# Three plain gate/up pairs a layer instead of four, with the low parts of three operand preparations made by ScalarE and adding DMAs, and weight chunks loaded several to a transfer

## The chip, the cores and the metric

The kernel runs on one core of a Trainium2 chip. The metric is the device time of one execution in microseconds (us), the median of several runs; less is better. The core has five engines that run side by side, each with an instruction stream of its own: TensorE (PE in the profile, with its weight loads as PEld), VectorE (DVE), ScalarE (ACT), GpSimd (POOL) and SyncE (SP). DMA queues move data between HBM and the on-chip memory SBUF. Plain loads are issued on SP. A DMA that adds into its destination (called an adding DMA here) is issued on POOL.

## What is computed

The reference is a decoder trunk of two layers in float32, on 512 tokens of 1024 features. Layer 0 mixes tokens by dilated attention, layer 1 by causal pooling. Each mixer is followed by a SwiGLU block, and this is where the change lies:

```
x = x + (silu(h @ w_gate) * (h @ w_up)) @ w_down      h = rmsnorm(x, g)
```

Here `h` is 512 x 1024, `w_gate` and `w_up` are 1024 x 2816 and `w_down` is 2816 x 1024. A last RMS norm ends the trunk.

## The kernel before

**Three products for one.** A float32 operand is kept as two tiles, a high part (the value rounded to the type that TensorE multiplies fast, `fp32r`) and a low part (the value minus its high part). A product of two such operands is three matmuls: high by high, high by low, low by high. Making the two parts is called splitting. The helper `split` (lines 90 to 92) makes the high part on ACT by a copy and the low part on DVE by a subtraction. Weights are split in the same way after they have been loaded, into tiles `w` (1024 columns) and `half` (512).

**Weights without DVE.** A weight unit of class `Plain` with `lean=True` is split without DVE: ACT makes the high part (line 139), ACT writes its negative into the low tile (line 140), and a DMA on POOL adds the weights once more from HBM into the low tile (line 143). So the weights are read twice.

**Two ways to do a gate/up pair.** The hidden width is 2816 = 22 x 128. For each of the 22 chunks `j` a gate product and an up product are made and combined to `silu(gate) * up`. A *plain* pair (`plain_pair`, line 1040) is two products of 8 steps, each of three matmuls with 512 columns: 48 matmuls. Its weights are two lean units. A *Strassen* pair (`strassen_pair`, with `chained`) treats gate and up together as a 2 x 2 block product with seven block products instead of eight: 7 products of 4 steps, each of three matmuls with 256 columns: 84 matmuls. Its weights are four tiles (`b`, `s`, `m`, `l`), split by `split` on ACT and DVE (line 92), after one adding DMA on POOL (line 168) and two additions on DVE (lines 184 and 185). It also reads sums and differences of blocks of `h`, which must be made first.

**Preparations.** These sums are made by `prepare(k)` (line 1055), for k = 0 to 3. `normed` forms the scaled rows in a tile `h` (two operations, line 570) and the differences in a tile `t` (lines 574, 575 and 577). Then three splits of 128 x 512 elements (line 92, written to `far`) and one of 128 x 256 with opposite sign (lines 95 and 96) give the operands. The tiles `h` and `t` are two `Temp` slots, and all four preparations use the same two. A preparation can overwrite them only when the previous one has read them. The first block product of a Strassen pair reads the operand `"11"`, the second `"1"`, for all four k in order. `"11"` comes from `h`, `"1"` and `"2"` from the first half of `t`, `"3"` and `"4"` from its second half.

**Order.** Each layer has `NPLAIN` = 4 plain pairs first, and `prepare(j)` stands in plain pair `j` between its gate and its up product. The table `PARTS` cuts the 22 chunks into parts of 2, 8, 8 and 4 chunks. After the first 2 chunks' pairs (and whatever plain pairs remain) come the down products of the first part: 8 products of 2 steps, 48 matmuls of 512 columns. Then come the Strassen pairs from `j` = 4 on. Weight loads and weight splits are queued in the order of use (`loads`, `steps`) and put out by `pump` as buffers come free: 5 tiles for split weights, 4 for raw ones. The instructions of each engine run in a fixed order, which a list scheduler chooses at build time by its own estimates of durations. An instruction that waits holds up all that stand behind it on its engine.

## Time and profile before

| | |
|---|---|
| median of 3 runs | 1192.59 us (1192.28 to 1192.77) |
| profiled execution, own time | 1192.39 us |
| its span in the trace | 1190.6 us |
| granted TensorE clock in the span | 0.999 |
| busy time PE, DVE, ACT, POOL | 1180.9, 961.6, 715.1, 201.8 us |

The span runs from the first instruction to the last, and the profiled execution's own time is 1.8 us longer. A row of a timeline gives start, duration, engine, line, operation, destination and sources, shape and count. Matmuls overlap in their pipeline, so that durations of single matmuls add up to more than the time: the distance from one start to the next is what one costs. The same holds, to a smaller degree, on DVE and ACT. "To landing" is the time from the issue of a DMA to its completion.

### The profile page before, as it was taken

How to read it: one execution, taken by the hardware profiler on the slowest of the kernel's cores; microseconds unless marked ns; L12 is line 12 of the kernel's file. 1: busy time of each engine (PE TensorE's matmuls, PEld its weight loads, DVE VectorE, ACT ScalarE, POOL GpSimd, SP SyncE). 2: the span in 40 equal slices, each digit the busy share in tenths (PEclk: the TensorE clock that was granted, in tenths of full speed). 3: DMA queues.
4: the chain of work that ended last, by engine and by line, in shares of the span. 5: the costliest groups of instructions: out<-in, count | busy, mean ns of one | idle time of the engine just before them, and what ended most of it. 6: DMA issues, size and time to landing. Idle time of an engine off the chain costs nothing.

```text
span 1190.6 us, 24964 instructions
## 1 busy us (share of the span) xinstructions
PE 1180.9 (99%) x9936; PEld 1119.4 (94%) x9936; DVE 961.6 (81%) x1682; ACT 715.1 (60%) x1247; POOL 201.8 (17%) x201
## 2 busy tenths in 40 slices
PE   9999999999999999999999999999999999999997
PEld 7889999999999988889999999988789999999997
DVE  6978798889788854699988988657779998898855
ACT  6445564455456545747756776676575776676563
POOL 1111211111111002411111111122450111111120
PEclk9999999999999999999999999999999999999999
DMA  8346666665766548957777777798595777777763
GB/s 276 127 102 164 155 155 162 170 158 149 191 144 163 155 141 209 196 105 200 191 191 192 195 201 195 192 265 206 116 196 112 192 196 200 193 192 195 194 135 96
DMA packets 83733, 207.30 MB, mean 174 GB/s; under 512 B 8464, under 2 KB 13728, under 8 KB 83616
## 3 DMA queue, kind: packets, MB, share of 16 engines
q1 hardware_dynamic: 51552, 141.98, 36.3%
q0 software_dynamic: 31920, 63.46, 32.3%
q8 instruction: 78, 1.28, 0.4%
q14 instruction: 39, 0.32, 0.1%
q10 hardware_dynamic: 144, 0.26, 0.1%
HBM read 203.57 MB, written 2.10 MB: 173 GB/s over the span
## 4 chain that ended last, share of the span: by engine, by line
PE 97%; issue 1%; DVE 1%; ACT 1%; POOL 0%; DVEq 0%; POOLq 0%
PE ps L453 19%; PE ps L455 19%; PE ps L454 19%; PE ps L321 8%; PE ps L322 8%; PE ps L324 8%; PE ps L624 2%; PE ps L626 2%; PE ps L625 2%; PE ps L914 2%; PE ps L836 1%; PE ps L708 1%; PE ps L830 1%; PE ps L728 1%; PE ps L894 0%
## 5 line engine op out<-in xcount | busy, mean ns | idle before, releaser
L91 ACT ACTIVATE w<-raw 128x1024 fp32r<-128x1024 f32 x261 | 276.2, 1063 | 169.5 <-PE ps L455 71.8
L92 DVE TENSOR_TENSOR w<-raw,w 128x1024 fp32r<-128x1024 f32 x261 | 317.8, 1221 | 50.0 <-ACT w L91 46.0
L453 PE MATMUL ps<-far,w 128*128 128x256 f32 x896 | 246.7, 275 | 0.5 <-ACT first L527 0.5
L454 PE MATMUL ps<-far,w 128*128 128x256 f32 x896 | 246.5, 275 | 0.0
L455 PE MATMUL ps<-far,w 128*128 128x256 f32 x896 | 246.5, 275 | 0.0
L453 PE MATMUL ps<-near,w 128*128 128x256 f32 x640 | 180.3, 282 | 0.0
L454 PE MATMUL ps<-near,w 128*128 128x256 f32 x640 | 177.0, 277 | 0.0
L455 PE MATMUL ps<-near,w 128*128 128x256 f32 x640 | 176.9, 276 | 0.0
L453 PEld LDWEIGHTS ps<-far,w 128*128 128x128 f32 x896 | 168.2, 188 | 1.0 <-ACT first L527 0.9
L454 PEld LDWEIGHTS ps<-far,w 128*128 128x128 f32 x896 | 168.2, 188 | 0.1
L455 PEld LDWEIGHTS ps<-far,w 128*128 128x128 f32 x896 | 168.2, 188 | 0.0
L322 PE MATMUL ps<-near,w 128*128 128x512 f32 (+1 forms) x332 | 125.0, 377 | 1.3 <-DVE near L386 1.3
L321 PE MATMUL ps<-near,w 128*128 128x512 f32 (+1 forms) x332 | 125.6, 379 | 0.0
L324 PE MATMUL ps<-near,w 128*128 128x512 f32 (+1 forms) x332 | 124.9, 376 | 0.0
L453 PEld LDWEIGHTS ps<-near,w 128*128 128x128 f32 x640 | 120.5, 188 | 0.4
L454 PEld LDWEIGHTS ps<-near,w 128*128 128x128 f32 x640 | 120.3, 188 | 0.0
L455 PEld LDWEIGHTS ps<-near,w 128*128 128x128 f32 x640 | 120.3, 188 | 0.0
L168 POOL DMA_DIRECT2D raw<-w_pair x36 | 43.5, 1208 | 296.0 <-DMA raw<-w_pair 113.6
L322 PEld LDWEIGHTS ps<-near,w 128*128 128x128 f32 x332 | 62.4, 188 | 12.9 <-DVE near L386 1.7
L321 PEld LDWEIGHTS ps<-near,w 128*128 128x128 f32 x332 | 62.3, 188 | 11.7 <-ACT near L91 0.4
L324 PEld LDWEIGHTS ps<-near,w 128*128 128x128 f32 x332 | 62.3, 188 | 11.5
L139 ACT ACTIVATE w<-raw 128x1024 fp32r<-128x1024 f32 x36 | 37.8, 1056 | 37.4 <-PE ps L324 35.4
(311 smaller groups left out, 2813.1 us busy)
## 6 DMA issues: line engine op xcount, KB each, us to landing
raw<-w_pair SPq DMA_DIRECT2D x80, 512.0 KB, 4.9
raw<-w_qkp SPq DMA_DIRECT2D x36, 512.0 KB, 4.4
raw<-w_pair POOLq DMA_DIRECT2D x36, 512.0 KB, 7.5
raw<-w_dblock SPq DMA_DIRECT2D x32, 512.0 KB, 4.6
raw<-w_v SPq DMA_DIRECT2D x18, 512.0 KB, 4.3
raw<-w_qkp POOLq DMA_DIRECT2D x18, 512.0 KB, 7.5
rawhalf<-w_pair SPq DMA_DIRECT2D x36, 256.0 KB, 5.1
raw<-w_dblock POOLq DMA_DIRECT2D x16, 512.0 KB, 7.4
```

The source lines that it names most:

```text
L91: nc.scalar.activation(hi, v, AF.Copy)
L92: nc.vector.tensor_tensor(lo, v, hi.bitcast(F32), op=OP.subtract)
L139: nc.scalar.activation(hi, self.raw.t[:, :self.n], AF.Copy)
L168: nc.gpsimd.dma_start(self.b.rearrange("p (a c) -> p a c", a=2), self.src[:, None, 3 * n:].to_broadcast([P, 2, n]), accum_op=OP.add)
L321: nc.tensor.matmul(self.p[:, cols], w[0][:, s], mh[:, cols], start=self.done == 0, stop=False)
L322: nc.tensor.matmul(self.p[:, cols], w[0][:, s], ml[:, cols], start=False, stop=False)
L324: nc.tensor.matmul(self.p[:, cols], w[1][:, s], mh[:, cols], start=False, stop=self.done == self.n)
L453: nc.tensor.matmul(dst, w.t[0][:, c], th, start=k == 0 and not on, stop=False, skip_group_check=on)
L454: nc.tensor.matmul(dst, w.t[0][:, c], tl, start=False, stop=False, skip_group_check=on)
L455: nc.tensor.matmul(dst, w.t[1][:, c], th, start=False, stop=k == n - 1, skip_group_check=on)
L624: nc.tensor.matmul(o, mh, wh, start=k == 0, stop=False)
L625: nc.tensor.matmul(o, mh, wl, start=False, stop=False)
```

## The change

Three things are changed together.

1. `NPLAIN` is 3. Chunk `j` = 3 becomes a Strassen pair, in both layers. The down products of the first part now follow plain pair 2, and the first Strassen pair, `j` = 3, follows them. Three plain pairs must host four preparations: `prepare(0)`, `prepare(1)` and `prepare(3)` stand in the plain pairs 0, 1 and 2, and `prepare(2)` is put at the end of plain pair 1.
2. In `prepare(1)`, `prepare(2)` and `prepare(3)` the three large splits are done by a new helper, `moved`: ACT makes the high part, ACT writes its negative into the low tile, and an adding DMA on POOL adds the value from its SBUF tile. `prepare(0)` and the small splits stay as they were.
3. Several weight chunks of `w_down` that lie in one unit are loaded by one transfer with a three-dimensional access pattern, and likewise added by one adding DMA. A unit of the first part has four chunks, a unit of the last part two.

```diff
-NPLAIN = 4
+NPLAIN = 3
...
+    def moved(hi, lo, v):
+
+        nc.scalar.activation(hi, v, AF.Copy)
+        nc.scalar.activation(lo, hi.bitcast(F32), AF.Copy, scale=-1.0)
+        nc.gpsimd.dma_start(lo, v.bitcast(F32R), accum_op=OP.add)
...
+        def views(self, t):
+            o = 0
+            for src in self.srcs:
+                q = src.shape[1] if len(src.shape) == 3 else 1
+                v = t[:, o:o + q * src.shape[-1]]
+                yield v.rearrange("p (q c) -> p q c", q=q) if len(src.shape) == 3 else v, src
+                o += q * src.shape[-1]
...
-            for src in self.srcs:
-                nc.sync.dma_start(self.raw.t[:, o:o + src.shape[-1]], src)
-                o += src.shape[-1]
+            for v, src in self.views(self.raw.t):
+                nc.sync.dma_start(v, src)
...
-                for src in self.srcs:
-                    nc.gpsimd.dma_start(lo[:, o:o + src.shape[-1]], src.bitcast(F32R), accum_op=OP.add)
-                    o += src.shape[-1]
+                for v, src in self.views(lo):
+                    nc.gpsimd.dma_start(v, src.bitcast(F32R), accum_op=OP.add)
...
-                        share(step, *[w_down[layer, q, :, o:o + n * P] for q in range(m, m + step)], lean=True,
+                        share(step, w_down[layer, m:m + step, :, o:o + n * P].rearrange("q p c -> p q c"), lean=True,
...
                 nc.vector.tensor_mul(gt, pg, row)
-                prepare(j)
+                prepare((0, 1, 3)[j])
                 pu = gu()
...
                 nc.vector.tensor_mul(up, up, gt)
+                if j == 1:
+                    prepare(2)
...
             def prepare(k):
+                parted = moved if k else split
                 h, t = normed(op, k, row, Temp(), Temp(), True)
...
-                split(b[:, 0].rearrange("p (a c) -> p a c", a=2), b[:, 1].rearrange("p (a c) -> p a c", a=2), hq[:, :, 0])
+                parted(b[:, 0].rearrange("p (a c) -> p a c", a=2), b[:, 1].rearrange("p (a c) -> p a c", a=2), hq[:, :, 0])
...
-                    split(b[:, 0], b[:, 1], t.t[:, i * S:(i + 1) * S])
+                    parted(b[:, 0], b[:, 1], t.t[:, i * S:(i + 1) * S])
```

More of the change, by code (lines that the diff above doesn't have):

```diff
@@ L123, in __init__ @@
         def __init__(self, *srcs, shift=0, lean=False):
-            self.srcs, self.n, self.w, self.shift, self.lean = srcs, sum(src.shape[-1] for src in srcs), None, shift, lean
+            self.srcs, self.n, self.w, self.shift, self.lean = srcs, sum(src.shape[-1] * (src.shape[1] if len(src.shape) == 3 else 1) for src in srcs), None, shift, lean
             loads.append((self, {"raw": 1}, self.load))
             steps.append((self, "w", self.split))
+        def views(self, t):
[5 more added lines that the diff above has]
+                o += q * src.shape[-1]
         def load(self):
             self.raw = Held("raw")
-            o = 0
-            for src in self.srcs:
-                nc.sync.dma_start(self.raw.t[:, o:o + src.shape[-1]], src)
-                o += src.shape[-1]
+            for v, src in self.views(self.raw.t):
+                nc.sync.dma_start(v, src)
         def split(self):
@@ L140, in split @@
                 nc.scalar.activation(lo, hi.bitcast(F32), AF.Copy, scale=-1.0)
-                o = 0
-                for src in self.srcs:
-                    nc.gpsimd.dma_start(lo[:, o:o + src.shape[-1]], src.bitcast(F32R), accum_op=OP.add)
-                    o += src.shape[-1]
+                for v, src in self.views(lo):
+                    nc.gpsimd.dma_start(v, src.bitcast(F32R), accum_op=OP.add)
             else:
```

## The prediction

> **What bounds the kernel now.** I read the page's head and its chain first, then the PE timeline around the stage that changes, then the stage by windows, then the streams of DVE, ACT and POOL in it.

> ```profile
> span 1190.6 us, 24964 instructions
> PE 1180.9 (99%) x9936; PEld 1119.4 (94%) x9936; DVE 961.6 (81%) x1682; ACT 715.1 (60%) x1247; POOL 201.8 (17%) x201
> PE 97%; issue 1%; DVE 1%; ACT 1%; POOL 0%; DVEq 0%; POOLq 0%
> ```

> The chain that ended last runs on PE for 97% of the span. Time is won by taking matmuls away, and lost where PE has to wait for something new. The next fence is the PE timeline of layer 0 at five places: the first matmul of plain pair 3, of the first down product, and of Strassen pairs 4, 5 and 6.

> ```profile
> 504.43 0.39 PE L321 MATMUL ps<-near,w 128*128 128x512 f32 x1
> 515.31 0.39 PE L321 MATMUL ps<-near,w 128*128 128x512 f32 x1
> 526.19 0.28 PE L453 MATMUL ps<-far,w 128*128 128x256 f32 x1
> 535.75 0.28 PE L453 MATMUL ps<-far,w 128*128 128x256 f32 x1
> 545.26 0.28 PE L453 MATMUL ps<-far,w 128*128 128x256 f32 x1
> ```

> A plain pair takes 515.31 - 504.43 = 10.88 us (48 matmuls, 0.2267 us each), the 48 down matmuls as much, and a Strassen pair 545.26 - 535.75 = 9.51 us (84 matmuls, 0.1133 us each, 9.52 us). PE has no gap here. The windows (busy time of PE, PEld, DVE, ACT and POOL, granted clock, DMA share, GB/s) show what stands beside it:

> ```profile
> 491.00:501.00 10.00, 10.00 (x45) 8.28 (x45) 10.00 (x19) 8.99 (x15) 5.30 (x6) 1.00 1.08 256
> 501.00:511.00 10.00, 10.00 (x45) 8.26 (x44) 9.97 (x18) 5.66 (x11) 4.83 (x5) 1.00 1.12 202
> 511.00:521.00 10.00, 10.00 (x46) 8.28 (x45) 10.00 (x19) 4.24 (x8) 1.21 (x1) 1.00 0.27 70
> 521.00:531.00 10.00, 10.00 (x67) 9.10 (x66) 9.59 (x18) 4.39 (x9) 0.00 (x0) 1.00 0.63 136
> ```

> DVE is as full as PE from 491 to 521 us. The DMA engines are full from 491 to 511 and mostly idle from 511 to 521.

> **Part 1: pair 3 as a Strassen pair.** 10.88 - 9.52 = 1.36 us less on PE, in two layers 2.72 us. This is the only gain on the path. Against the profiled execution's 1192.39 us it gives 1189.67 us; the runs' median stands 0.20 us above that execution, so 1189.9 us for the median.

> The price is time for preparation. Before, the last preparation had to be ready at 526.19, after the down products. Now the first Strassen pair starts 10.88 us earlier, at 515.3. DVE and ACT in the stage:

> ```profile
> 494.00 1.40 DVE L570 SCALAR_TENSOR_TENSOR temp<-x,nrm,row 128x512 f32<-128x512 f32 x2
> 495.92 0.68 DVE L574 TENSOR_TENSOR temp<-temp 128x512 f32<-128x512 f32 x1
> 496.52 0.68 DVE L92 TENSOR_TENSOR far<-temp,far 128x512 fp32r<-128x512 f32 x1
> 497.12 0.41 DVE L575 TENSOR_TENSOR temp<-temp 128x256 f32<-128x256 f32 x1
> 514.27 1.29 DVE L92 TENSOR_TENSOR far<-temp,far 128x512 fp32r<-128x512 f32 x2
> 491.20 1.14 ACT L91 ACTIVATE far<-temp 128x512 fp32r<-128x512 f32 x2
> 480.67 2.01 ACT L139 ACTIVATE w<-raw 128x1024 fp32r<-128x1024 f32 x2 [7.06 <-PE ps L324]
> ```

> `prepare(1)` began at 494.00 and the last split of `prepare(3)` ended at 515.56, on a DVE that never paused. That is just about when it is needed now, so DVE load decides whether all four fit:

> ```profile
> L92 DVE TENSOR_TENSOR w<-raw,w 128x1024 fp32r<-128x1024 f32 x261 | 317.8, 1221 | 50.0 <-ACT w L91 46.0
> L184 DVE TENSOR_TENSOR raw<-raw 128x512 f32<-128x512 f32 x81 | 55.4, 684 | 1.6 <-issue 1.2 <-DVE qk L508 0.2
> L92 DVE TENSOR_TENSOR far<-temp,far 128x512 fp32r<-128x512 f32 x24 | 15.9, 684 | 0.0
> ```

> The Strassen pair brings DVE three weight splits of 1.22, one half as large (0.68), two additions of 0.68 and five small operations of 0.41: 7.8 us. The plain pair took three of 0.68 with it, so +5.8 us a layer. **Part 2** takes nine subtractions of 0.684 away: -6.2 us. Together -0.4 us: DVE's load stays, and its work for the preparations shrinks by 6.2 us, so the mere DVE work is done some 5 us before PE needs it. ACT gains nine copies (1.14 / 2 = 0.57 each, 5.1 us a layer); it loses four weight copies and gets 3.5. It was 5.66 of 10 us busy from 501 to 511, which hides them at no cost; without that cover, a high and a low copy more in the chain is 1.1 us.

> **The new wait.** The low part is complete only when its DMA has landed, and `h` and `t` can't be overwritten before. So `prepare(2)` and `prepare(3)` on DVE wait for DMAs of the one before. Behind the waiting operation on DVE stand the low part of act 1, the splits of pair 3's weights and the down additions; the down products wait for the first, pair 3 for the second. With L for the time from issue to landing, the longest chain goes through `t`:
> - L574 of `prepare(1)` at 495.9. The two halves of `t` need 0.94 us on DVE (0.60 and 0.34, start to start) until the first is whole; two high and two low copies on ACT take 2.28 us. The last DMA is issued 3.2 us after L574 and lands L later; only then can L574 of `prepare(2)` run. The same again for `prepare(3)`.
> - There the first half of `t` needs 0.94 + 1.14 = 2.1 us and L to be an operand: 495.9 + 2 x 3.2 + 2.1 + 3L = 504.4 + 3L.
> - PE reads it (operand `"1"`, k = 3) one product (1.36 us) and three of four steps (1.02 us) after 515.3: at 517.7.

> So nothing is lost up to L = 4.43 us, and 3 (L - 4.43) us a layer above it. The chain through `h` (1.4 + 1.14 + L a round, from 494.0, needed at 516.3) allows 4.9. Nearest rows, adding DMAs from HBM in three windows: 256 KB at the end of layer 1, 256 and 512 KB near 470 us, and 128 KB in this stage:

> ```profile
> L143 POOL DMA_DIRECT2D w<-w_down x5: 860/1208/1249, 1148.8 to 1157.3; - x5
> DMA to landing us min/median/max: 4.1/5.6/6.4
> L143 POOL DMA_DIRECT2D w<-w_pair x3: 877/890/1217, 468.2 to 473.6; - x3
> DMA to landing us min/median/max: 4.9/5.8/7.7
> L143 POOL DMA_DIRECT2D w<-w_down x8: 860/1504/2463, 496.3 to 505.2; - x8
> DMA to landing us min/median/max: 6.9/7.1/7.6
> q0 software_dynamic: 2692, 4.21, 51.0%
> ```

> The ends are 4.1 us (nothing queued ahead) and 7.1 us (DMA share above 1). At 4.1 the chain ends at 516.7, 1.0 us early: no cost. At 7.1 it ends at 525.7: 8.0 us a layer. I take 4.1 to 4.4, the emptier end, because what filled the queues goes or moves: pair 3's lean units leave with 1 MB of adding DMAs, and the down weights are added earlier (below). From 480 to 530 us the software queue moved 4.21 MB in 51% of 50 us, 165 GB/s, so one of the nine 256 KB transfers is 1.6 us, and they come some 3 us apart. That nothing comes from HBM could shorten L below 4.1; no row shows it, and it would gain nothing more. Against it speak the weight loads of pair 5, which start near 503 and share the engines with the last six; both ends go into the range.

> [...]

> **POOL, and part 3.** POOL's stream in the stage:

> ```profile
> 488.95 1.21 POOL L168 DMA_DIRECT2D raw<-w_pair  x1 [2.28 <-DMA raw<-w_pair]
> 496.27 3.66 POOL L143 DMA_DIRECT2D w<-w_down  x4 [2.83 <-ACT w L140]
> 503.52 4.12 POOL L143 DMA_DIRECT2D w<-w_down  x4
> 518.88 1.21 POOL L168 DMA_DIRECT2D raw<-w_pair  x1 [11.24 <-DVE x L1166]
> ```

> Four adding DMAs cost POOL 3.66 us; one with four chunks I put between 1.2 (L168, two chunks) and 3.66. It falls from 8 issues to 2 a layer in the first part and 8 to 4 in the last; SP likewise. POOL and SP aren't on the chain, so this is worth nothing by itself; it makes room for nine issues of 0.86 to 1.2 us. The moved issues stand in POOL's order beside L168, which waits for its load (2.28 us at 488.95): one such wait ahead of a moved DMA adds to L. The down units' high copies take the slot that pair 3's unit had (480.67), so their sums land near 484 + 7.6 = 492 where 504.4 is needed; without that cover PE would lose at most the 7.1 us once a layer.

> **The rivals.**
> 1. *The adding DMAs land a little late.* L between 4.45 and 5.3: half or all of the gain goes, at L = 4.9 (least of the second landing row) 3 x 0.47 = 1.4 us a layer, 1192.7 us in all. For it: nine transfers share a queue with pair 5's loads. Against it: the share of 0.27.
> 2. *They land late, and it is slower.* From L = 4.88 on it costs more than it brings, and over 0.2% from 5.3. At the first window's median of 5.6: 3.5 us a layer, +4.3 net, 1196.9 us; at 7.1, 16.0 - 2.7 = +13.3, 1205.9 us. For it: the medians of all three windows lie above 5.3. Against it: those DMAs came in pairs and fours behind each other.
> 3. *Issue is stretched while DVE works.* Single issues in this stage took up to 2463 ns against 860: 1.6 us more in each of three links, a chain end at 504.4 + 3 x 5.7 = 521.5, 3.8 us a layer, 1197.5 us. But four issues took 3.66 us together beside a full DVE, so the 2463 is one behind another. [...]
> 4. *The change doesn't do what it says*: DVE, blocked in order, becomes the bound; 3 us of blocking costs up to 3 us a layer, 1195.9 us. Against it: the 6.2 us won.

> **How the numbers follow.** Forecast, all hidden: 0.45, 1189.9 us, its own range 1189.3 to 1190.2. Rival 1: 0.27, between 1190.2 and 1195.0. Rival 2: 0.20. Rivals 3 and 4 together: 0.08. The measurement can tell about 0.2% (2.4 us) from no change, and the whole gain is 2.72 us, so the forecast alone is faster: 0.45 faster, 0.27 same, 0.28 slower. The range of 8 in 10 goes from 1189.3 to 1198.0: it holds rival 3 and rival 2 up to L = 5.75.

> **What would show it.** Right: pair 3's first 256-column matmul near 515.3 in layer 0, no gap on PE in the 10 us behind it, a landing median of the DMAs from `temp` under 4.5 us, DVE never idle for `temp` by more than 3 us. Wrong: PE waiting for `far` in the first Strassen pair, or DVE's L570 or L574 waiting for a DMA while down additions stand behind it.

## The result, and the profile after

The changed kernel takes 1211.26 us (median of 4 runs, 1208.99 to 1211.73), the kernel before beside it 1192.43 us. The ratio is 1.0156, with a 95% interval of 1.0144 to 1.0168: slower by 18.8 us, where 2.5 us of gain were forecast and the range ended at 1198.0. The profiled execution took 1211.73 us.

Lines of the page of the changed kernel: span, busy times, the shares of the chain that ended last, PE's busy tenths and its granted clock in 40 slices, and one group of matmuls.

```profile
span 1209.9 us, 25095 instructions
...
PE 1187.3 (98%) x10008; PEld 1128.0 (93%) x10008; DVE 961.9 (80%) x1680; ACT 727.2 (60%) x1273; POOL 202.6 (17%) x195
...
PE   9999999999999999979999999999997999999997
...
PEclk9999999999999999979999999999998999999999
...
PE 90%; issue 3%; DMA 3%; DVE 2%; ACT 1%; POOL 0%; DVEq 0%; POOLq 0%; SPq 0%
...
L464 PE MATMUL ps<-far,w 128*128 128x256 f32 x944 | 263.7, 279 | 13.5 <-DMA far<-temp 13.5
```

The chain was 97% PE and is 90%; two slices have a lower PE and a lower clock, one in each layer's first Strassen pair. In the last line, the matmuls of a high by a low part (L464), PE stood idle for 13.5 us until DMAs from `temp` had landed. The next rows are PE's timeline there: first matmul of pair 3 in layer 0, two waits in it, and one in layer 1. (Lines stand ten to thirteen further down than before: L463 to L465 are the Strassen matmuls, L580 and L584 the preparation's steps on DVE that were L570 and L574, L96 to L98 the new `moved`, L178 the adding DMA of a pair's weights that was L168.)

```profile
515.68 0.39 PE L463 MATMUL ps<-far,w 128*128 128x256 f32 x1 [0.27 <-DVE x L1179]
521.61 0.58 PE L464 MATMUL ps<-far,w 128*128 128x256 f32 x1 [4.50 <-DMA far<-temp]
527.37 0.58 PE L464 MATMUL ps<-far,w 128*128 128x256 f32 x1 [2.83 <-DMA far<-temp]
916.16 0.58 PE L464 MATMUL ps<-far,w 128*128 128x256 f32 x1 [5.97 <-DMA far<-temp]
```

Pair 3 starts on time (515.68, forecast 515.3), runs to its fourth step and stands still for low parts that haven't landed. The windows of layer 0 (length, busy time of PE, PEld, DVE, ACT, POOL, granted clock, DMA share, GB/s) show a second loss behind the first:

```profile
504.00:515.60 11.60, 11.41 (x51) 9.11 (x49) 8.65 (x16) 5.22 (x11) 4.26 (x4) 1.00 0.65 124
515.60:521.60 6.00, 1.44 (x10) 1.24 (x10) 4.08 (x7) 2.21 (x3) 1.20 (x1) 0.78 1.07 193
521.60:524.20 2.60, 2.59 (x12) 2.59 (x12) 2.60 (x6) 1.76 (x4) 0.20 (x1) 0.50 0.28 113
...
527.40:532.60 5.20, 5.20 (x24) 5.20 (x25) 1.92 (x5) 1.06 (x3) 0.32 (x1) 0.50 0.60 154
532.60:542.00 9.40, 9.40 (x85) 9.40 (x84) 8.15 (x15) 6.64 (x12) 0.89 (x1) 1.00 0.71 162
```

Behind the waits PE runs at a granted clock of 0.50: 24 matmuls in 5.20 us, 0.217 each instead of 0.113. It is back at 1.00 only at 532.6. DVE stands idle too, for DMAs that still read the two temporary tiles:

```profile
503.50 1.41 DVE L580 SCALAR_TENSOR_TENSOR temp<-x,nrm,row 128x512 f32<-128x512 f32 x2 [3.60 <-DMA far<-temp]
513.01 1.42 DVE L580 SCALAR_TENSOR_TENSOR temp<-x,nrm,row 128x512 f32<-128x512 f32 x2 [2.95 <-DMA far<-temp]
520.21 0.69 DVE L584 TENSOR_TENSOR temp<-temp 128x512 f32<-128x512 f32 x1 [1.92 <-DMA far<-temp]
```

That is 8.5 us of idle DVE in a stage where it had next to none before; layer 1 has 8.5 us of the same waits.

To compare runs I use one sum, **PE's loss**: from the PE timeline of 480 to 680 us (layer 0) and 850 to 1080 us (layer 1), the start-to-start distances beyond 0.227 us (512 columns) and 0.113 us (256 columns), less the 0.3 and 1.8 us that the kernel before shows in the same stretches (1.4 of the 1.8 is one wait at 852 us that the kernel with part 3 alone doesn't have). The changed kernel lost 12.1 us in layer 0 and 10.2 in layer 1. With the 2.72 us that the Strassen pairs do save, the sum is 12.1 + 10.2 - 2.7 = 19.6; the span grew by 19.3. So the difference lies, to within 0.4 us, in these two stretches. Of the 12.1, 7.8 are the two waits and some 3.9 the half clock (2.6 and 5.2 us at half rate).

### The profile page after: what moved, and what is told of

Same layout as the page of the kernel before. It is cut to its first block, busy times and chain, and to the rows that moved or that the text cites. A ratio compares the mean times of both kernels' runs of the same rounds, so it can differ in the third digit from the quotient of the medians.

```text
span 1209.9 us, 25095 instructions
## 1 busy us (share of the span) xinstructions
PE 1187.3 (98%) x10008; PEld 1128.0 (93%) x10008; DVE 961.9 (80%) x1680; ACT 727.2 (60%) x1273; POOL 202.6 (17%) x195
## 3 DMA queue, kind: packets, MB, share of 16 engines
q8 instruction: 78, 1.28, 0.4%
## 4 chain that ended last, share of the span: by engine, by line
PE 90%; issue 3%; DMA 3%; DVE 2%; ACT 1%; POOL 0%; DVEq 0%; POOLq 0%; SPq 0%
PE ps L463 20%; PE ps L464 19%; PE ps L465 19%; PE ps L331 6%; PE ps L332 6%; PE ps L334 6%; DMA far<-temp 2%; PE ps L634 2%; PE ps L635 2%; PE ps L636 2%; PE ps L924 2%; PE ps L846 1%; PE ps L718 1%; DVE temp L580 1%; PE ps L738 1%
## 5 line engine op out<-in xcount | busy, mean ns | idle before, releaser
L91 ACT ACTIVATE w<-raw 128x1024 fp32r<-128x1024 f32 x267 | 282.6, 1063 | 152.6 <-PE ps L465 71.2
L92 DVE TENSOR_TENSOR w<-raw,w 128x1024 fp32r<-128x1024 f32 x267 | 325.3, 1222 | 49.0 <-ACT w L91 44.8
L464 PE MATMUL ps<-far,w 128*128 128x256 f32 x944 | 263.7, 279 | 13.5 <-DMA far<-temp 13.5
L463 PE MATMUL ps<-far,w 128*128 128x256 f32 x944 | 263.1, 279 | 1.4 <-ACT first L537 1.2
L465 PE MATMUL ps<-far,w 128*128 128x256 f32 x944 | 262.7, 279 | 0.0
L464 PEld LDWEIGHTS ps<-far,w 128*128 128x128 f32 x944 | 180.5, 191 | 14.5 <-DMA far<-temp 14.5
L463 PEld LDWEIGHTS ps<-far,w 128*128 128x128 f32 x944 | 180.3, 191 | 2.6 <-ACT first L537 1.9
L465 PEld LDWEIGHTS ps<-far,w 128*128 128x128 f32 x944 | 180.5, 191 | 0.0
L463 PE MATMUL ps<-near,w 128*128 128x256 f32 x640 | 180.3, 282 | 0.0
L464 PE MATMUL ps<-near,w 128*128 128x256 f32 x640 | 177.0, 277 | 0.0
L465 PE MATMUL ps<-near,w 128*128 128x256 f32 x640 | 176.9, 276 | 0.0
L463 PEld LDWEIGHTS ps<-near,w 128*128 128x128 f32 x640 | 120.5, 188 | 0.4
L464 PEld LDWEIGHTS ps<-near,w 128*128 128x128 f32 x640 | 120.3, 188 | 0.0
L465 PEld LDWEIGHTS ps<-near,w 128*128 128x128 f32 x640 | 120.3, 188 | 0.0
L331 PE MATMUL ps<-near,w 128*128 128x512 f32 (+1 forms) x300 | 113.2, 378 | 0.0
L332 PE MATMUL ps<-near,w 128*128 128x512 f32 (+1 forms) x300 | 112.6, 375 | 0.2 <-DVE near L396 0.2
L334 PE MATMUL ps<-near,w 128*128 128x512 f32 (+1 forms) x300 | 112.5, 375 | 0.0
L178 POOL DMA_DIRECT2D raw<-w_pair x38 | 45.8, 1204 | 281.9 <-DMA raw<-w_pair 102.1
L332 PEld LDWEIGHTS ps<-near,w 128*128 128x128 f32 x300 | 56.4, 188 | 10.8 <-DVE near L396 0.7
L331 PEld LDWEIGHTS ps<-near,w 128*128 128x128 f32 x300 | 56.3, 188 | 10.4 <-ACT near L91 0.4
L334 PEld LDWEIGHTS ps<-near,w 128*128 128x128 f32 x300 | 56.3, 188 | 10.1
L91 ACT ACTIVATE half<-rawhalf 128x512 fp32r<-128x512 f32 x83 | 52.3, 631 | 15.6 <-PE ps L465 13.5
```

Of the source, the lines that this page charges most:

```text
L91: nc.scalar.activation(hi, v, AF.Copy)
L92: nc.vector.tensor_tensor(lo, v, hi.bitcast(F32), op=OP.subtract)
L178: nc.gpsimd.dma_start(self.b.rearrange("p (a c) -> p a c", a=2), self.src[:, None, 3 * n:].to_broadcast([P, 2, n]), accum_op=OP.add)
L331: nc.tensor.matmul(self.p[:, cols], w[0][:, s], mh[:, cols], start=self.done == 0, stop=False)
L332: nc.tensor.matmul(self.p[:, cols], w[0][:, s], ml[:, cols], start=False, stop=False)
L334: nc.tensor.matmul(self.p[:, cols], w[1][:, s], mh[:, cols], start=False, stop=self.done == self.n)
```

## The experiments

Three theories at the start. **A**: the low parts land late, because each preparation waits on DVE until the adding DMAs have read the temporary tiles of the one before. **B**: what lacks is the 10.88 us of cover, whoever writes the low parts. **C**: part 3's larger transfers do it. All results but that of the idle times of known length, which stands in its section, in one table (median in us, ratio to the kernel before on the same chip with its 95% interval, PE's loss in both layers):

| kernel | median | ratio | loss |
|---|---|---|---|
| changed kernel | 1211.26 | 1.0156 (1.0144 to 1.0168) | 12.1, 10.2 |
| part 3 alone | 1191.73 | 0.9994 (0.9984 to 1.0004) | 0, -1.4 |
| three plain pairs, all low parts on DVE | 1194.65 | 1.0020 (1.0011 to 1.0030) | 2.4, 2.8 |
| four plain pairs with the adding DMAs | 1214.98 | 1.0187 (1.0172 to 1.0202) | 9.8, 11.9 |
| changed, four temporary tiles | 1205.36 | 1.0105 (1.0090 to 1.0120) | 10.8, 6.0 |
| changed, fillers on PE | 1213.09 | 1.0174 (1.0159 to 1.0189) | 3.9, 4.0, and 8.2 each of fillers |
| GpSimd subtracts, three preparations | 1203.00 | 1.0088 (1.0072 to 1.0105) | 8.5, 6.5 |
| GpSimd subtracts, two preparations | 1200.38 | 1.0068 (1.0053 to 1.0083) | 7.4, 4.9 |
| adding DMAs for preparation 3 alone | 1200.14 | 1.0063 (1.0048 to 1.0078) | 1.1, 10.2 |
| changed, higher priority | 1208.15 | 1.0133 (1.0118 to 1.0148) | 12.1, 7.9 |
| all on DVE, one weight tile by DMA | 1191.59 | 0.9992 (0.9983 to 1.0002) | 0.8, 0.9 |
| the same, again | 1192.18 | 0.9997 (0.9987 to 1.0006) | 0.9, 1.8 |
| the same, two weight tiles | 1191.73 | 1.0000 (0.9991 to 1.0009) | 1.3, 0.9 |
| all on DVE, four weight tiles by DMA | 1203.81 | 1.0096 (1.0079 to 1.0113) | 7.9, 6.7 |

### Part 3 alone

```
-NPLAIN = 3
+NPLAIN = 4
...
-                prepare((0, 1, 3)[j])
+                prepare(j)
...
-                if j == 1:
-                    prepare(2)
...
-                parted = moved if k else split
+                parted = split
```

> The kernel before with part 3 alone (several chunks a transfer). Theories A and B: no difference, 1192.0 to 1193.0. Theory C: most of the loss, 1200 or more.

1191.73 us, and no loss on PE: theory C falls. Loading several chunks with one transfer cost nothing here and brought nothing that can be measured (0.9994, 0.9984 to 1.0004).

### Three plain pairs, all low parts on DVE

```
-                parted = moved if k else split
+                parted = split
```

> Three plain pairs, but all low parts subtracted by DVE as before (no moved); part 3 stays. Theory A (the low parts land late: each preparation waits on DVE for the adding DMAs that still read the two temporary tiles of the one before, and PE waits for the last to land): no DVE wait for a DMA from temp is left, DVE has 6.2 us more work, so PE waits 0 to 2.5 us a layer and the clock stays at full: 1189.9 to 1195. Theory B (the 10.88 us that a plain pair gave as cover are missing, whoever writes the low parts): PE waits 6 us a layer or more in the first Strassen pair, 1203 or more. Theory C (the chunked transfers do it): about 1211, as after.

1194.65 us, 16.6 us under the changed kernel. Without `moved` three plain pairs nearly fit, so theory B, with its 6 us a layer, falls. But the gain isn't there either: PE loses 2.4 and 2.8 us. A window of layer 0 (columns as above) and the largest wait, in layer 1:

```profile
500.00:510.00 10.00, 10.00 (x46) 8.26 (x45) 10.00 (x19) 4.42 (x9) 0.00 (x0) 1.00 0.03 4
```

```profile
900.39 0.50 PE L331 MATMUL ps<-near,w 128*128 128x512 f32 x1 [1.85 <-DVE u L1059]
```

DVE is busy 10.00 of 10 us and PE waits for DVE's results. DVE has no room, and that decides how the next run is read.

### Four plain pairs with the adding DMAs

```
-NPLAIN = 3
+NPLAIN = 4
...
-                prepare((0, 1, 3)[j])
+                prepare(j)
...
-                if j == 1:
-                    prepare(2)
```

> Four plain pairs, each preparing one operand as before, with the low parts of preparations 1 to 3 by ScalarE and adding DMAs, and the chunked transfers. Need of PE: 528.5 us in layer 0 instead of 517.7; the changed kernel's last DMA landed at 527.3. Theory A: DVE still idles 2 to 4 us for the DMAs, but PE waits 0 to 1 us a layer: 1192 to 1195. Theory B: 1192 to 1193. Theory C: 1200 or more.

1214.98 us, the slowest of the real variants, although PE needs the operands 10.9 us later. Theory A as I had put it expected 1192 to 1195 and is wrong in its second half. A window, a DVE row, and PE's waits of layer 0:

```profile
500.00:510.00 10.00, 10.00 (x46) 8.29 (x45) 1.41 (x2) 2.61 (x4) 4.26 (x4) 1.00 1.04 190
```

```profile
508.28 1.41 DVE L580 SCALAR_TENSOR_TENSOR temp<-x,nrm,row 128x512 f32<-128x512 f32 x2 [8.44 <-DMA far<-temp]
```

```profile
526.38 0.50 PE L331 MATMUL ps<-near,w 128*128 128x512 f32 x1 [1.43 <-DVE u L1059]
...
535.03 0.39 PE L463 MATMUL ps<-far,w 128*128 128x256 f32 x1 [2.07 <-ACT first L537]
541.30 0.40 PE L463 MATMUL ps<-far,w 128*128 128x256 f32 x1 [1.64 <-ACT first L545]
```

No wait of a matmul is put down to a DMA here. These three, a fourth of 1.92 us at 529.96 for which the profile names no releaser, and one stretch at half clock (0.83 on the mean from 530 to 540 us) make up most of the 9.8. DVE does wait for DMAs, 8.44 us at once and 12.7 in layer 0 (the other two waits are 3.13 and 1.11), with 1.41 of 10 us busy where it was full; everything behind L580 in its order comes late, and with it what PE waits for: two of its waits name copies by ScalarE, one a step of DVE. So theory A has to be put differently, as **A2**: the loss is the time for which DVE, full and in order, is held by adding DMAs; late low parts are only one of the places where it reaches PE.

### The changed kernel with four temporary tiles

```
-NEAR = 11
+NEAR = 9
...
-OPEN = 2
+OPEN = 4
...
-            order = loose
+            order = loose[temps[0] % OPEN:] + loose[:temps[0] % OPEN]
...
             self.i, t = slot("temp", F32)
+            temps[0] += 1
```

> The changed kernel with four temporary tiles taken in turn instead of two (two fewer tiles for operands beside them). In layer 0 two of the four are occupied by the layer's input, so the waits stay as they are; in layer 1 preparation 2 no longer waits for the DMAs of preparation 1, and preparation 3 only for those of 1. Theory A: layer 0 as in the changed kernel (some 12 us lost); in layer 1 the last low part is issued near 909 and lands 913 to 917 where 912 is needed: 0 to 5 us lost instead of 11.3, in all 1200 to 1206. Theory B, and a theory that the DMAs are slow whatever waits for them: layer 1 loses as much as before, 1210 to 1212.

1205.36 us. In layer 0, where the waits had to stay, DVE waits 8.0 us for DMAs from `temp` and the loss stays (10.8). In layer 1 these waits fall from 8.5 us to none and the loss from 10.2 to 6.0 (by the sum used here the 11.3 of the expectation is 10.2). Taking away the wait gives back part of the time: that speaks for A and A2. What is left of layer 1 is another wait, seen in POOL's timeline and PE's:

```profile
904.22 1.22 POOL L178 DMA_DIRECT2D raw<-w_pair  x1 [3.11 <-DVE u L1062]
904.95 2.30 POOL L98 DMA_DIRECT2D far<-temp  x2
```

```profile
913.35 0.58 PE L464 MATMUL ps<-far,w 128*128 128x256 f32 x1 [3.37 <-DMA far<-temp]
```

POOL, in order as well, waited 3.11 us (the trace names a step of DVE) before it issued the adding DMA of a pair's weights. The two moved DMAs behind it were issued at 904.95 and 905.50, behind these 512 KB in the queue, and landed 8.4 and 9.1 us later.

### The changed kernel with a higher priority for the preparations

```
+        with tc.high_priority():
+            nc.scalar.activation(hi, v, AF.Copy)
+            nc.scalar.activation(lo, hi.bitcast(F32), AF.Copy, scale=-1.0)
+            nc.gpsimd.dma_start(lo, v.bitcast(F32R), accum_op=OP.add)
```

> The changed kernel with the copies and adding DMAs of the three preparations given a higher priority in the planner that sets the order. In layer 0 the order of POOL stays as it is; in layer 1 the adding DMA of the second half of preparation 2 moves ahead of the 512 KB adding DMA for a pair's weights, behind which it landed 8.7 us after its issue. Theory A (the landing behind that transfer is the largest single piece of the chain): it lands in 4 to 5 us, the chain in layer 1 is 3 to 4 us shorter and so is PE's wait: 1206 to 1209. Rival (the links between the landings, not this one, hold the chain): 1210 to 1213.

1208.15 us, inside theory A's range, though its interval still overlaps the changed kernel's a little. The moved DMA now stands ahead of the 512 KB one and lands in 6.5 us instead of 8.7; DVE waits 3.15 us for it instead of 5.55. But the next moved DMA took the place behind the 512 KB, landed after 9.6 us, and PE's wait of 5.98 us in layer 1 is as long as before, where theory A expected 3 to 4 us less. The queueing was moved, not removed. The 2.3 us by which the loss of layer 1 fell come from behind that wait: two smaller waits are gone and the half clock lasts 6.8 us there instead of 10.2. So the number was hit, and not by the mechanism that theory A gave for it.

### Adding DMAs for preparation 3 alone

```
-                parted = moved if k else split
+                parted = moved if k == K2 - 1 else split
```

> The changed kernel with adding DMAs for preparation 3 alone: nothing is written into its temporary tiles afterwards, so DVE waits for no DMA, and the low parts only have to land in time. Theory A: DVE's work falls 2.05 us a layer below that of three plain pairs with all by DVE; the DMAs are issued at 511 to 513 and land at 515 to 520 where PE needs them at 516.7 to 517.9: PE waits 0 to 3 us a layer, 1190 to 1196. Rival (the landing alone is the loss, not DVE's blocked order): as much as in the changed kernel, 5 us a layer or more, 1200 or more.

1200.14 us, a time that the rival had named, but the layers part. Layer 0: the loss is 1.1 us, less than with all on DVE (2.4); DVE waits for no DMA and has less to do. Layer 1, PE's timeline:

```profile
906.78 0.58 PE L464 MATMUL ps<-far,w 128*128 128x256 f32 x1 [6.36 <-DMA far<-temp]
```

Two of the three DMAs stand behind a 512 KB one again and land 9.0 and 9.6 us after their issue. So both parts of the mechanism exist by themselves: DVE's wait, without which layer 0 is well, and the landing behind a weight transfer, which in layer 1, where DVE waits for no DMA, costs 10.2 us with what follows it.

### GpSimd subtracts instead

```
     def moved(hi, lo, v):

         nc.scalar.activation(hi, v, AF.Copy)
-        nc.scalar.activation(lo, hi.bitcast(F32), AF.Copy, scale=-1.0)
-        nc.gpsimd.dma_start(lo, v.bitcast(F32R), accum_op=OP.add)
+        nc.gpsimd.tensor_tensor(lo, v, hi.bitcast(F32), op=OP.subtract)
```

> The changed kernel with the low parts of preparations 1 to 3 subtracted by GpSimd itself (POOL, one TENSOR_TENSOR each, no DMA). Such an operation on POOL took 1.55 us elsewhere in this kernel where a landing takes 3.3 to 8.7. Theory A: POOL needs 13.9 us for nine, done near 515; DVE's waits for the temporary tiles fall under 1.5 us each; PE waits 0 to 2 us a layer: 1189.5 to 1194. Rival (not the landing, but any third engine that DVE has to wait for, or POOL beside a full DVE slowing both): 1198 or more.

A second kernel did so for preparations 1 and 2 only (`parted = moved if 0 < k < K2 - 1 else split`).

> As with GpSimd subtracting, but for preparations 1 and 2 only; preparation 3, the last and urgent one, goes to DVE as before. Theory A: POOL's six subtractions (9.3 us) are done near 510; no DMA wait, DVE 4.1 us a layer less loaded than with all on DVE: 1189.5 to 1192, at or under the kernel before. Rival (POOL beside a full DVE slows both): 1195 or more.

1203.00 and 1200.38 us: the rival is right in both. Groups of instructions from 490 to 520 us, by shape (count, busy time, mean ns), first of the kernel with part 3 alone, then of the one where GpSimd subtracts for three:

```profile
L580 DVE SCALAR_TENSOR_TENSOR temp<-x,nrm,row 128x512 f32<-128x512 f32 x6 | 4.2, 746 | 0.0
L102 DVE SCALAR_TENSOR_TENSOR far<-temp,far 128x256 fp32r<-128x256 f32 x4 | 1.7, 419 | 0.0
```

```profile
L579 DVE SCALAR_TENSOR_TENSOR temp<-x,nrm,row 128x512 f32<-128x512 f32 x6 | 6.3, 1088 | 0.0
L101 DVE SCALAR_TENSOR_TENSOR far<-temp,far 128x256 fp32r<-128x256 f32 x4 | 3.9, 967 | 0.0
...
L97 POOL TENSOR_TENSOR far<-temp,far 128x512 fp32r<-128x512 f32 x9 | 15.8, 1770 | 6.9 <-ACT far L96 6.9
```

The same operations of DVE take 1088 ns instead of 746 and 967 instead of 419 while GpSimd works: from 500 to 510 us DVE is "busy" 10.00 of 10 us with 11 operations where it did 17. The time saved on DVE comes back as longer instructions. DVE's operations with one input in PSUM kept their 674 to 681 ns.

### What the half clock costs

First attempt: keep PE at work in the two idle places of the changed kernel.

```
+            if fill and k == n - 1:
+                p = ps()
+                for i in range(fill):
+                    nc.tensor.matmul(p[:, :H2], w.t[0][:, :P], T[name, 0][0], start=i == 0, stop=i == fill - 1)
```

> The changed kernel with 36 matmuls of 256 columns into a spare bank (4.1 us at full clock, results unused) ahead of the last step of products "11" and "1" of the first Strassen pair of each layer, the two places where PE stood idle. The landings set the end there, so the idle time itself stays lost. Theory A with the clock as a part of its own (PE's idle gaps halve its clock, and the matmuls behind the last landing then run at half rate): clock 1.00 throughout, 2.5 to 4 us a layer come back, 1203 to 1207. Rival (the low clock costs nothing, because PE waits in any case): 1210 to 1213.

1213.09 us, which is no answer: the clock did not stay at 1.00. In layer 0 the fillers closed the two waits, but another one opened right behind them, which the trace puts down to a copy by ScalarE:

```profile
528.38 0.39 PE L467 MATMUL ps<-far,w 128*128 128x256 f32 x1 [1.79 <-ACT first L541]
```

and from 529.9 to 533.2 us the matmuls ran at half rate all the same. So I measured the clock in the kernel before, with idle times of known length:

```
+                if gap:
+                    p, zero = ps(), fpool.tile([P, P], F32R, tag="zero", name="zero", bufs=1)
+                    nc.tensor.matmul(p[:, :H2], T["11", 0][0][:, :P], T["11", 0][0], start=True, stop=True)
+                    nc.scalar.activation(zero, p[:, :P], AF.Copy, scale=0.0)
+                    for i in range(gap - 1):
+                        nc.scalar.activation(zero, zero.bitcast(F32), AF.Copy)
...
+        if zero is not None:
+            nc.tensor.matmul(dst, zero, T[name, 0][0], start=True, stop=False)
```

> The kernel before with PE made to stand idle once in six Strassen pairs (7, 11 and 15 of each layer) for growing lengths: a small matmul, a chain of 1, 4, 8, 12, 16 or 20 ScalarE copies that ends in a tile of zeros, and the pair's first matmul waits for it and adds zero (also one more such matmul in two later products). Theory (an idle gap costs itself, and from some length on also a stretch at half clock): gaps under about 2 us cost themselves, longer ones 1.5 to 4.5 us more each, with PE at 0.2125 us a matmul for 3 to 9 us after the gap. Rival (the half clock in the changed kernel came from the repeated waits, not from one gap): every gap costs itself alone, clock 1.00. In all 15 to 40 us over the kernel before, of which the gaps themselves some 15 to 25.

1230.16 us. Three of the six waits in PE's timeline, and windows behind them:

```profile
634.99 0.38 PE L452 MATMUL ps<-far,zero 128*128 128x256 f32 x1 [1.92 <-ACT zero L1133]
...
677.72 0.39 PE L452 MATMUL ps<-far,zero 128*128 128x256 f32 x1 [3.89 <-ACT zero L1133]
...
955.12 0.58 PE L452 MATMUL ps<-far,zero 128*128 128x256 f32 x1 [5.41 <-ACT zero L1133]
```

```profile
635.00:640.00 5.00, 5.00 (x43) 5.00 (x44) 2.33 (x4) 1.11 (x3) 0.00 (x0) 1.00 0.90 165
677.70:679.00 1.30, 1.28 (x11) 1.28 (x12) 0.81 (x4) 0.42 (x1) 0.00 (x0) 1.00 1.02 162
679.00:682.80 3.80, 3.80 (x22) 3.80 (x21) 0.38 (x1) 0.57 (x2) 0.22 (x1) 0.55 0.66 232
955.10:958.90 3.80, 3.78 (x17) 3.78 (x18) 0.22 (x1) 0.37 (x1) 1.21 (x1) 0.50 0.32 113
```

Idle times of 1.28 and 1.92 us cost themselves. Those of 3.89, 5.41, 6.01 and 8.14 us were each followed by 3.1 to 4.3 us of matmuls at half clock, 1.6 to 2.2 us lost beyond the gap. So the rival (single gaps cost themselves alone) falls, and my 1.5 to 4.5 us was too high for single gaps. Sum: 26.7 idle + 7.3 half clock + 2.7 for 24 small matmuls = 36.7 of the 37.8 us by which the median grew. The length of the gap alone doesn't decide, though: in the fillers' run the half clock followed a gap of 1.79 us, and here none followed one of 1.92. What it went with can be read from the times at which the granted clock changes. In each trace they stand on a grid of 3.41 us: in the changed kernel at 518.93, 532.58 (4 steps later), 914.87 (116 steps after the first) and 925.11 us (119). Windows cut along this grid, two from the fillers' run and then two from this one:

```profile
526.42:529.84 3.42, 1.63 (x14) 1.46 (x13) 1.62 (x4) 0.95 (x3) 0.00 (x0) 1.00 0.82 216
529.84:533.25 3.41, 3.41 (x18) 3.41 (x18) 0.42 (x1) 0.87 (x2) 1.21 (x1) 0.50 0.07 12
```

```profile
631.21:634.62 3.41, 1.86 (x17) 1.65 (x15) 3.34 (x6) 3.03 (x7) 1.20 (x1) 1.00 0.56 192
634.62:638.04 3.42, 3.05 (x26) 3.05 (x27) 2.71 (x5) 0.68 (x2) 0.01 (x1) 1.00 0.70 85
```

The fillers' gap lay within one step of the grid; PE was busy for 1.63 us of it, 48%, and the next step ran at half clock. The gap of 1.92 us fell across two steps, busy for 54% and 89%, and neither was followed by half clock. All 16 traces agree: each of the 23 steps at full clock that was followed by one at half had PE busy for at most 48%, and only three below 50% (47, 49 and 49%) were not. At half clock a step busy for 80% or less was followed by another, one busy for 86% or more by full clock. So in these runs the half clock went with PE's busy share in steps of 3.41 us; a step needn't be idle for it, as the one busy for 48% shows. A step at half clock full of matmuls lost about half its length, 1.7 us (0.217 us a matmul instead of 0.113), and the drop came at the end of the step, here after PE had resumed (at 678.99, where PE had resumed at 677.72).

In the changed kernel two waits a layer, or one and smaller ones behind it, keep the clock at half for four steps in layer 0, 518.93 to 532.58 us. PE was at work in 7.8 us of them (2.6 + 5.2), which is the 3.9 us above.

### Relieving DVE without holding its tiles

If A2 is right, three plain pairs need a little less work on DVE that no one has to wait for. The low part of a weight tile can come from HBM itself, so that no temporary tile is held.

```
         def blocks(self):
-            self.take("b", "w", self.a)
+            if not self.lean:
+                return self.take("b", "w", self.a)
+            n = 2 * self.n
+            self.w["b"] = w = Held("w", self.shift)
+            w.n = self.n
+            hi, lo = (t[:, :n] for t in w.t)
+            nc.scalar.activation(hi, self.a, AF.Copy)
+            nc.scalar.activation(lo, hi.bitcast(F32), AF.Copy, scale=-1.0)
+            nc.gpsimd.dma_start(lo, self.src[:, self.n:3 * self.n].bitcast(F32R), accum_op=OP.add)
...
-                parted = moved if k else split
+                parted = split
...
-                    pairs(w_pair[layer, j], shift=0, back=True)
+                    pairs(w_pair[layer, j], shift=0, back=True, lean=j < NPLAIN + 1)
```

> Three plain pairs with all preparations on DVE, and the low part of the first weight tile of the first Strassen pair of each layer by ScalarE and an adding DMA from HBM (nothing waits for a temporary tile): DVE 1.22 us a layer less. Theory (three plain pairs fail because DVE has no room, and every us taken from DVE in this stage is a us on PE): 1 to 2.4 us less than with all on DVE, 1192 to 1193.7. Rival (what holds PE there is not DVE's load): 1194 to 1195.5.

1191.59 us, 3.1 under all on DVE for 2 x 1.22 us of work taken off it (the two stood on different chips; their losses differ by 3.5). That is more than the 1 to 2.4 us expected. DVE's load is what held that version, and a microsecond of it is about a microsecond on PE (2.5 us for 2.44 with the repeat below). With `lean=j < NPLAIN + 4`:

> The same for the first weight tile of the first four Strassen pairs of each layer: DVE 4.9 us a layer less in the 40 us behind the preparations. Theory (DVE's load): most of the 2.7 us of the Strassen pair comes through, 1189.5 to 1192. Rival (more adding DMAs in the one software queue land late, weights now): PE waits for w, 1195 or more.

1203.81 us: the rival. PE's timeline and the landing times of the four DMAs in layer 0:

```profile
529.35 0.58 PE L474 MATMUL ps<-far,w 128*128 128x256 f32 x1 [4.27 <-DMA w<-w_pair]
```

```profile
DMA to landing us min/median/max: 7.9/9.2/10.9
```

The first pair's DMA left 20 us ahead of its use; the second one was issued 7 us ahead, behind a 512 KB adding DMA, landed 10.9 us later, and PE waited for it. The one DMA of layer 0 in the version before stood behind 512 KB too and took 7.5 us; it did no harm because it had left 19 us ahead. Then once more with one tile, and with the pair's last, half tile as well:

> The version with all preparations on DVE and the first weight tile of the first Strassen pair completed by an adding DMA, once more with more rounds, beside the next one. Its first ratio was 0.9992 with an interval of 0.9983 to 1.0002; PE's excess over full rate left in it against the kernel before is 0.7 us in layer 0 and 0.9 us in layer 1, so 2.7 - 1.6 = 1.1 us of gain should be there: a ratio of 0.9985 to 0.9997, with an interval that ends under 1. Rival (nothing beats the kernel before): 0.9998 to 1.0005.

> The same, with the low part of the pair's last, half weight tile (256 KB) by an adding DMA too: DVE 0.68 us a layer less. Theory (DVE's load is what is left of the loss): up to 0.7 us a layer less than with one tile, 1190.0 to 1191.4. Rival (each further adding DMA lands late or holds up the others in the software queue, as with four pairs): 1192 or more.

1192.18 and 1191.73 us, ratios 0.9997 and 1.0000 with intervals that hold 1. The first stands on the border of both expectations, but its interval doesn't end under 1; the second lies between its two. The last 0.68 us of relief bring nothing measurable. So a version with three plain pairs reaches the kernel before, and none of these is shown to beat it: of the 2.7 us, 1.7 to 2.7 go again in small waits in the three runs. What makes them up isn't settled.

## Why the prediction was wrong

**Part 1, right.** The Strassen pairs are worth 2.72 us: losses and gain add up to the span within 0.4 us, and pair 3 began 0.4 us from the forecast place.

**The sum, wrong in its links.** The step that failed is "504.4 + 3L". The 3.2 us from L574 to the issue of the last DMA became 5.8. L itself was near what was taken for most (3.3 to 4.8 us for six of the nine DMAs of layer 0), and 5.2 to 7.2 for three that shared the DMA engines with a weight transfer. Rows of DVE, of POOL, and landings (the DMAs issued at 502.25, 512.99 and 524.00, in this order):

```profile
496.40 0.69 DVE L584 TENSOR_TENSOR temp<-temp 128x512 f32<-128x512 f32 x1
507.17 0.68 DVE L584 TENSOR_TENSOR temp<-temp 128x512 f32<-128x512 f32 x1
```

```profile
502.25 0.86 POOL L98 DMA_DIRECT2D far<-temp  x1 [0.93 <-ACT w L91]
...
512.28 1.22 POOL L178 DMA_DIRECT2D raw<-w_pair  x1 [1.21 <-DMA raw<-w_pair]
512.99 1.44 POOL L98 DMA_DIRECT2D far<-temp  x1
...
524.00 0.91 POOL L98 DMA_DIRECT2D far<-temp  x1 [6.46 <-DVE x L1179]
```

```profile
DMA to landing us min/median/max: 3.9/3.9/3.9
DMA to landing us min/median/max: 7.2/7.2/7.2
DMA to landing us min/median/max: 3.3/3.3/3.3
```

| step of layer 0 | taken | measured |
|---|---|---|
| first L574 (now L584) | 495.9 | 496.40 |
| to its last issue | 3.2 | 5.85 |
| landing | 4.1 to 4.4 | 3.9 |
| to the next L584 | 0 | 1.02 |
| to its last issue | 3.2 | 5.82 |
| landing | 4.1 to 4.4 | 7.2 |
| to the third L584 | 0 | 0.03 |
| to the issue of "1" | 2.1 | 3.79 |
| landing | 4.1 to 4.4 | 3.3 |
| operand whole | 516.7 to 517.6 | 527.33 |

Against the 516.7 that I worked out with L = 4.1, the links, the first step and the pauses between cost 8.5 us and the landings 2.1. I had added up the durations of the chain's own instructions. Each of them stood in an order with others: ScalarE's copies behind a split, POOL's issue behind L178, which waited 1.21 us for its load, DVE's step behind a weight split. The prediction named the last but one ("one such wait ahead of a moved DMA adds to L") and gave it no price; it cost twice, as a later issue and as 512 KB ahead in the queue. The lower bounds of such a chain are sums of durations; the expected value is not.

The chain through `h`, for which the prediction had more room (L up to 4.9), failed first, and for the same reason. L580 writes `h`, and its waits of 3.60 and 2.95 us, 6.5 of DVE's 8.5, ended when the first DMA of the preparation before had landed: issued at 499.16 and 506.78, landed after 4.23 and 6.12 us, the second beside a 512 KB weight load. From L580 to the issue took 5.2, 3.3 and 3.3 us where 1.4 + 1.14 = 2.5 were taken. The operand `"11"` of the last preparation was whole at 521.57 instead of 516.3, and that is PE's first and longest wait in layer 0 (4.50 us); `"1"` made the second (2.83 us).

**"DVE's load stays", the wrong measure.** The work was as counted, 6.2 us less a layer for the preparations. But DVE was idle for 8.5 us instead, more than it won. Rival 4 had this mechanism, priced it at "up to 3 us a layer" and set the 6.2 us won against it; the run with four plain pairs shows it at its purest, 12.7 us of idle DVE and 9.8 us lost on PE, with no wait of PE put down to a DMA. The four tiles (layer 1) and the version with preparation 3 alone (layer 0) show that without the wait the loss goes in part or nearly whole.

**Rival 2, the right direction, too small.** It counted 3(L - 4.43) and nothing for the links or for what a waiting PE does afterwards. With the three landings measured (14.4 us together) it gives 1.1 us a layer, so that slower came out is not to its credit. The half clock adds some 3.9 us in layer 0, a third of the loss there, and no row of the trace before showed it: PE's longest wait in the two stretches was 1.26 us there (at 852.05), and the clock stayed at 1.00.

**Parts right.** Part 3 is worth nothing by itself (0.9994). POOL's single issues took 0.86 to 1.45 us in layer 0, so rival 3 didn't occur. The signs named for a failure, PE waiting for `far` and L570 or L574 waiting for a DMA, are the ones that came. But two signs named for being right came as well: pair 3's start, and a landing median from `temp` under 4.5 us (4.2). The median was no test of the chain.

**The chances.** 0.20 for rival 2 was low for a chain of three waits whose limit lay 0.03 to 0.33 us a link above the value taken: with 1.0 us of room in all, any one piece of order on any of four engines used it up.

## What to carry to other kernels

Before an operation is moved off a full in-order engine, ask what that engine will then wait for: the DMAs that read its scratch tiles here kept those tiles until they had landed (DVE's waits of 3.60, 2.95 and 1.92 us in layer 0 of the changed kernel), and such waits can cost PE about their length (12.7 us of waits and 9.8 lost in layer 0 of the run with four plain pairs), whatever work was saved. The relief that did no harm here had a source that the engine doesn't write again and was issued far ahead: 19 us ahead, 512 KB before it in the queue didn't matter (landed after 7.5 us), 7 us ahead they did (10.9 us). Price a chain over several engines with the neighbours in each engine's order, and add the half clock where waits may leave PE as little busy as it was here before each drop, at most 48% of a step of 3.41 us (some 3.9 us of the loss in layer 0 of the changed kernel).

## What was unexpected of the hardware

```profile
DMA to landing us min/median/max: 3.3/4.2/7.2
```

- Beside subtractions of GpSimd (1.77 us each) DVE's operations with two SBUF inputs took 1.09 us instead of 0.75, and 0.97 instead of 0.42.
